# Routing ahead of an expert gather: eight choices taken early, sums of squares moved to VectorE, one head's weights moved behind

## The chip, the cores and the metric

The kernel runs on one core of a Trainium2 chip. Its engines are TensorE (matmuls; PE in the profile, its weight loads PEld), VectorE (DVE), ScalarE (ACT), GpSimd (POOL) and SyncE (SP). 16 DMA engines move data between HBM and SBUF; transfers are issued by SP, ACT and POOL. The metric is the device time of one execution in microseconds, lower is better; the kernel before has a median of 1541.05 us over three runs.

## The reference

One sequence of 256 tokens of width 1024 passes a first block (modulated norm, windowed attention beside a short convolution, then a PEER expert layer) and a second part with two attention layers and two gated feed-forward layers. All is float32. The change concerns the expert layer, `peer`, whose core is:

```python
qh = (t @ w_q).reshape(T, PEER_HEADS, 2, PEER_KEY_DIM // 2)
s = jnp.einsum('thpd,hpnd->thpn', qh, sub_keys)
s_top, i_top = lax.top_k(s, PEER_TOPK)
cand = s_top[:, :, 0, :, None] + s_top[:, :, 1, None, :]
best, pos = lax.top_k(cand.reshape(T, PEER_HEADS, 256), PEER_TOPK)
idx = take_along_axis(cand_idx, pos); g = softmax(best)
ue, ve = u_tab[idx], v_tab[idx]
act = gelu(einsum('thkd,td->thk', ue, t))
return einsum('thk,thkd->td', g * act, ve)
```

Here `t` is `h2 = rmsnorm(x, n2) * (1 + sc2) + sh2`, there are 8 heads, and each token picks 16 of 16384 experts for each head. Every pick needs a row of `u` and a row of `v`, 1024 floats each.

## The kernel before

The 256 tokens are two tiles of 128 (t = 0, 1). `phase_a` computes the first block up to the residual, `phase_b` the experts, `phase_c` the rest. A scheduler puts each engine's instructions in an order when the program is built; the order in the source is a priority, and `tc.issue_after(ins)` keeps what stands inside it behind `ins` on that engine's queue.

In `phase_b` a step `s` of 16 is one head for one token tile, and it has 16 choices `k`. So there are 256 choices, each one an indirect DMA issued by POOL (`fetch`, line 934): for each of 128 tokens it gathers one row of 8 KB, `u` and `v` side by side, into a place of a ring of `NR` = 13 places of 8 KB a partition (tag `uv`). `first` (line 939) takes the dot product of the `u` half with the tokens `ht` on VectorE and a GELU on ScalarE; `second` (line 948) scales an identity matrix by activation and softmax weight on VectorE (`dgw`) and adds the `v` half to four PSUM banks with eight products on TensorE. After `second` the place in the ring is free for the gather 13 choices on.

Before a step's choices stand, its indices are needed. `query(h)` projects the normed tokens `hf` with the head's weights `wq[h]` (`project`) and multiplies by the head's keys (`keys`). `routing(s)` then runs on VectorE in four steps: the best 16 of 128 scores for each half (`half`, with MAX8, FIND_INDEX8 and MATCH_REPLACE8, eight at a time), the best 16 of the 256 sums (`pairs`) and the decoding of their numbers into expert indices `IX[s]` (`decode`). In the loop of line 974 the steps of `routing(s + 2)` are dealt out at every fourth choice.

Head 0 goes a shorter way (`query_early`, line 848): its projection is made from `xg`, the tokens times the gain, before the norm is known; the scores are then scaled by the norm `rs` (its squares are summed in PSUM by 16 products with a column of ones in `square_sums`), and the shift's part, 16 products of the weights with the modulation column, then four with the keys, is added. `normed` builds `hf` with the norm spread over partitions (`spread`), `rows` transposes it into `ht`.

The weights of heads 0 to 3 are loaded into ring places ahead of any gather, those of heads 4 to 7 into stage buffers `raw`, `whi`, `wlo` (`qload`, line 773). All are issued on SP in turn. Queries 1 to 3 stand ahead of the loop, 4 to 7 at choices 8, 36, 68, 100; at choice 104 the prefetch of phase c's weights is allowed, at 120 `angles`, a small computation for phase c.

## Time and profile before

| | us |
|---|---|
| median of three runs | 1541.05 (1534.71 to 1544.97) |
| the profiled execution | 1528.92 |
| its span, first to last instruction | 1527.1 |
| TensorE busy / VectorE busy | 1384.6 / 1161.1 |
| ScalarE busy / POOL busy | 601.3 / 353.0 |
| mean granted clock of TensorE | 0.991 |

The busy share of an engine is taken over a program of stages with different limits, so it doesn't say what sets the time in a given stage. The page's row of DMA rates over 40 slices shows it better: slices 8 to 24 (some 270 to 920 us) move 376 to 427 GB/s, those of phase c mostly 100 to 200. The rows of a window are best read side by side: what each engine was busy, and what the DMA engines moved.

### The profile page before, as it was taken

The page shows a single profiled execution, that of the slowest core. Times are in us where ns is not written, and L with a number is a line of the kernel's source. Part 1 is how long each engine was busy: PE and PEld are TensorE (multiplying, and loading weights), DVE is VectorE, ACT ScalarE, POOL GpSimd, SP SyncE. Part 2 cuts the span into 40 slices and gives each one's busy share as a digit, 9 for nine tenths or more (in the row PEclk, how much of TensorE's full clock was granted, in tenths as well). Part 3 has the DMA queues.
Part 4 walks back from the last instruction along what each step waited for, and adds up shares of the span by engine and source line. Part 5 has one row for each costly group of instructions (what it writes and reads, how often), then busy time and mean ns, then how long its engine had stood idle before and what let it go on. Part 6 is the DMA issues. An engine that isn't in the chain of part 4 may idle for free.

```text
span 1527.1 us, 28521 instructions
## 1 busy us (share of the span) xinstructions
PE 1384.6 (91%) x10892; PEld 1294.2 (85%) x10892; DVE 1161.1 (76%) x2692; ACT 601.3 (39%) x1223; POOL 353.0 (23%) x316
## 2 busy tenths in 40 slices
PE   7999996999988887888688889999999999999998
PEld 7988896988987777777677779989999996899997
DVE  3887775996897779776565658876988888588885
ACT  1646633312111113111010005775655568555553
POOL 0000001343455455555455530000000000000000
PEclk9999998999999999999999999999999999999999
DMA  9677766999999999999999994434655543355550
GB/s 326 230 261 225 245 204 252 413 396 405 376 426 426 426 426 426 426 427 426 425 427 425 427 411 156 147 122 159 198 192 182 190 153 97 116 189 193 184 189 28
DMA packets 82839, 433.40 MB, mean 284 GB/s; under 512 B 9296, under 2 KB 10448, under 8 KB 49680
## 3 DMA queue, kind: packets, MB, share of 16 engines
q0 software_dynamic: 37120, 269.24, 42.4%
q1 hardware_dynamic: 43712, 159.67, 31.2%
q10 hardware_dynamic: 1872, 2.68, 0.5%
q8 instruction: 86, 1.41, 0.4%
q14 instruction: 49, 0.40, 0.1%
HBM read 430.51 MB, written 1.05 MB: 283 GB/s over the span
## 4 chain that ended last, share of the span: by engine, by line
PE 51%; DMA 31%; DVE 12%; issue 4%; ACT 1%; POOL 0%; SPq 0%; DVEq 0%; POOLq 0%; ACTq 0%
PE b L135 50%; DMA uv<-in_uv,IX 27%; DVE uv L944 2%; DMA rawx<-in_wmodT 1%; DVE wlo L212 1%; DVE dgw L953 1%; DMA rawx<-in_wmod 1%; DVE s L815 1%; DVE wlox L212 1%; DMA raw<-in_wmodT 1%; DMA raw<-in_wqkv 1%; DVE e L648 0%; DVE oh L916 0%; DVE rawx L477 0%; DVE SI L817 0%
## 5 line engine op out<-in xcount | busy, mean ns | idle before, releaser
L135 PE MATMUL b<-dgw,uv 128*128 128x128 f32 x4096 | 506.7, 279 | 98.9 <-DVE dgw L953 98.6
L135 PEld LDWEIGHTS b<-dgw,uv 128*128 128x128 f32 x4096 | 473.2, 192 | 133.7 <-DVE dgw L953 131.9
L944 DVE CUSTOM_DVE_ANT_0 uv<-uv,ht 128x1024 f32<-128x1024 f32 x256 | 312.7, 1221 | 142.1 <-DMA uv<-in_uv,IX 141.8
L936 POOL DMA_INDIRECT uv<-in_uv,IX x256 | 328.9, 1285 | 330.2 <-DMA uv<-in_uv,IX 141.6
L135 PE MATMUL b<-H,whi 128*128 128x256 f32 x1296 | 244.8, 287 | 2.7 <-DVE mx L1042 1.4
L945 ACT ACTIVATE act<-act 128x1 f32<-128x1 f32 x256 | 51.5, 202 | 496.7 <-DVE act L944 492.8
L135 PE MATMUL b<-H,wlox 128*128 128x256 f32 x824 | 231.9, 281 | 0.0
L135 PE MATMUL b<-H,whix 128*128 128x256 f32 x1216 | 222.9, 282 | 2.2 <-DVE H L535 1.1
L135 PEld LDWEIGHTS b<-H,whi 128*128 128x128 f32 x1296 | 201.6, 189 | 9.1 <-issue 5.0
L135 PEld LDWEIGHTS b<-H,whix 128*128 128x128 f32 x1216 | 187.8, 188 | 6.7 <-issue 3.2
L135 PEld LDWEIGHTS b<-H,wlox 128*128 128x128 f32 x824 | 155.6, 189 | 0.7 <-issue 0.3
L135 PE MATMUL b<-H,wlo 128*128 128x256 f32 x440 | 122.4, 288 | 0.0
L212 DVE TENSOR_TENSOR wlox<-rawx,whix 128x1024 fp32r<-128x1024 f32 x60 | 73.1, 1223 | 35.4 <-ACT whix L203 34.6
L953 DVE TENSOR_SCALAR dgw<-cn,act,we 128x128 f32<-128x128 f32 x256 | 88.0, 344 | 13.1 <-ACT act L945 13.1
L203 ACT ACTIVATE whix<-rawx 128x1024 fp32r<-128x1024 f32 x60 | 63.0, 1058 | 77.2 <-PE b L135 60.9
L203 ACT ACTIVATE whi<-rawx 128x1024 fp32r<-128x1024 f32 x59 | 62.3, 1059 | 66.2 <-PE b L135 61.3
L357 POOL TENSOR_TENSOR rs<-ms,nhalf 128x2 f32<-128x2 f32 x6 | 6.2, 1034 | 349.4 <-DVE ms L355 349.4
L212 DVE TENSOR_TENSOR wlox<-raw,whix 128x1024 fp32r<-128x1024 f32 x57 | 69.7, 1222 | 18.3 <-ACT whix L203 17.6
L135 PEld LDWEIGHTS b<-H,wlo 128*128 128x128 f32 x440 | 82.5, 189 | 1.2 <-issue 0.7
L203 ACT ACTIVATE whi<-raw 128x1024 fp32r<-128x1024 f32 x58 | 60.9, 1056 | 54.1 <-PE b L135 42.7
L203 ACT ACTIVATE whix<-raw 128x1024 fp32r<-128x1024 f32 x57 | 60.3, 1058 | 50.8 <-PE b L135 48.1
L1257 DVE SCALAR_TENSOR_TENSOR c<-u,cl,c 128x256 f32<-128x256 f32 x176 | 73.8, 479 | 0.8 <-ACT c L1254 0.7
(340 smaller groups left out, 2236.2 us busy)
## 6 DMA issues: line engine op xcount, KB each, us to landing
rawx<-in_wup SPq DMA_DIRECT2D x45, 512.0 KB, 3.5
raw<-in_wup SPq DMA_DIRECT2D x43, 512.0 KB, 3.5
raw<-in_wdn SPq DMA_DIRECT2D x23, 512.0 KB, 3.4
rawx<-in_win SPq DMA_DIRECT2D x21, 512.0 KB, 4.5
rawx<-in_wdn SPq DMA_DIRECT2D x21, 512.0 KB, 3.4
rawx<-in_wmodT SPq DMA_DIRECT2D x18, 512.0 KB, 4.5
raw<-in_wmodT SPq DMA_DIRECT2D x14, 512.0 KB, 4.4
raw<-in_win SPq DMA_DIRECT2D x13, 512.0 KB, 4.3
```

What stands on the lines that cost most here:

```text
L135: return self.nc.tensor.matmul(out, lhsT, rhs, start=start, stop=stop).ins
L203: nc.scalar.activation(hi[:], raw[:], AF.Copy)
L212: nc.vector.tensor_sub(u.lo[:], u.raw[:], u.hi[:].bitcast(F32))
L357: nc.gpsimd.tensor_tensor(rs[:], ms[:], self.nhalf[:, 0:2], OP.pow)
L815: nc.vector.match_replace(s2[:], v[:, 0:8], s, -3e38)
L936: nc.gpsimd.indirect_dma_start(out=g[:], out_offset=None, in_=A["uv"], in_offset=bass.IndirectOffsetOnAxis(ap=IX[s][:, k:k + 1], axis=0))
L944: dot = nc.vector.tensor_tensor_reduce(u, u, ht[:, t, :], 1.0, 0.0, OP.mult, OP.add, accum_out=a[:, 0:1]).ins
L945: nc.scalar.activation(a[:, 1:2], a[:, 0:1], AF.Gelu)
L953: done = nc.vector.tensor_scalar(dg[:], self.con("ident"), a[:, 1:2], e[:, k:k + 1], op0=OP.mult, op1=OP.mult).ins
L1257: nc.vector.scalar_tensor_tensor(c[:, a, :], u[:, a, j:j + 256], self.col("cw2", at + 44 * j), c[:, a, :], op0=OP.mult, op1=OP.add)
```

## The change

- `query_early` is put in another order: the shift's 16 products come first, and the projection is queued behind them. The squares are taken on ScalarE as before, but summed over four pairs of feature tiles by VectorE, so that 4 products with the column of ones remain of 16. Scaling by the norm and adding the shift are one VectorE instruction for each token tile, and the norm is spread here.
- `first8` (new) takes eight choices of step 0 from the best 8 of each half: 64 sums instead of 256. The first eight gathers use its indices, in the same order of choices. Then come `normed`, `rows`, and the rest of routing(0), which does not repeat the first MAX8 and FIND_INDEX8 of the halves; gathers 8 to 12 follow, then routing(1).
- `top8` and `parts` are split off `top16` and `decode`.
- Heads 0 to 2 have their weights in the ring, heads 3 to 6 in the stage buffers. Head 7 is loaded at choice 36, into the `raw` and `whi` that head 3 had. Queries 1 and 2 stand ahead of the loop, 3 to 7 at choices 8, 36, 68, 100, 132. The prefetch is allowed at 136 and `angles` at 144. The keys of head 1 are issued from ACT instead of POOL.
- A pad of 224 bytes stands in the pool below the ring. With the 32 bytes of the new tile `IX8` the ring's start moves by 256 bytes, from byte 111360 of a partition to 111616, which is a multiple of 512.

```diff
+            def qplace(h):
+                if h < 3:
                     g = rows_.tile([P, 2 * D], F32, name="wq", tag="uv", bufs=NR)
+                    wq[h] = [g[:, 0:D], g[:, D:2 * D]]
+                    return g
+                wq[h] = [self.slot("r", w, F32, "st") for w in
+                         ("wlo" if h == 6 else "raw", "wlo" if h == 6 else "whi")]
+            def qload(h, g=None):
+                if g is not None:
                     self.take(g[:].rearrange("p (u c) -> p u c", u=2), A["wpq"][2 * h:2 * h + 2].rearrange("u p c -> p u c"))
-                    wq[h] = [g[:, 0:D], g[:, D:2 * D]]
-                else:
-                    wq[h] = []
-                    for u in (2 * h, 2 * h + 1):
-                        g = self.slot("r", ["raw", "whi", "raw", "whi", "raw", "whi", "wlo", "wlo"][u - 8], F32, "st")
-                        self.take(g[:], A["wpq"][u])
-                        wq[h].append(g[:])
+                    return
+                for u in range(2):
+                    self.take(wq[h][u][:], A["wpq"][2 * h + u])
+            places = {h: qplace(h) for h in (0, 1, 2)}
             self.inturn = True
-            for h in range(8):
-                qload(h)
+            for h in range(7):
+                if h >= 3:
+                    qplace(h)
+                qload(h, places.get(h))
...
             def query_early():
-                ps = project(0, xg)
-                sums = self.square_sums(x)
-                rs = self.rms_col(sums)
-                sc, ks, end = keys(0, ps)
                 pc = self.rot("mm")
-                with self.tc.issue_after(end):
-                    for a in range(2):
-                        for k in range(KT):
-                            self.mm(pc[:, a * 128:a * 128 + 128], wq[0][a][:, k * 128:k * 128 + 128],
-                                    self.mod[:, 24 + k:25 + k].to_broadcast([P, 128]), k == 0 and a == 0, k == KT - 1 and a == 1)
+                for a in range(2):
+                    for k in range(KT):
+                        end = self.mm(pc[:, a * 128:a * 128 + 128], wq[0][a][:, k * 128:k * 128 + 128],
+                                      self.mod[:, 24 + k:25 + k].to_broadcast([P, 128]), k == 0 and a == 0, k == KT - 1 and a == 1)
                 cb = wk.tile([P, 256], F32, name="cb", tag="s2256", bufs=1)
                 nc.scalar.activation(cb[:], pc[:, 0:256], AF.Copy)
+                sq = [wk.tile([P, 512], F32, name="sq", tag=t, bufs=n) for t, n in [("oh", 1), ("qT", 2), ("qT", 2)]]
+                for b in range(4):
+                    q = sq[b] if b < 2 else sq[2]
+                    nc.scalar.activation(q[:], x[:, 2 * b:2 * b + 2, :].rearrange("p a t -> p (a t)"), AF.Square)
+                    if b:
+                        nc.vector.tensor_tensor(sq[0][:], sq[0][:], q[:], OP.add)
+                with self.tc.issue_after(end):
+                    ps = project(0, xg)
+                sums = self.rot("tr")
+                for h in range(2):
+                    for t in range(2):
+                        self.mm(sums[:, t:t + 1], sq[0][:, h * 256 + t * 128:h * 256 + t * 128 + 128], self.con("ones", 1),
+                                h == 0 and t == 0, h == 1 and t == 1)
+                rs = self.rms_col(sums)
+                ks = wk.tile([P, 256], F32, name="ks", tag="ks", bufs=2)
+                nc.gpsimd.dma_start(ks[:], A["keysT"][0])
                 pb = self.rot("mm")
                 for a in range(2):
                     self.mm(pb[:, a * 128:a * 128 + 128], cb[:, a * 128:a * 128 + 128], ks[:, a * 128:a * 128 + 128])
+                sc, _, _ = keys(0, ps, ks)
+                sb = wk.tile([P, 256], F32, name="sb", tag="cd", bufs=1)
+                nc.scalar.activation(sb[:], pb[:, 0:256], AF.Copy)
+                self.spread(rs, bc[:])
                 for t in range(2):
                     c = slice(t * 256, t * 256 + 256)
-                    nc.scalar.activation(scores[0][:, c], sc[:, c], AF.Copy, scale=rs[:, t:t + 1])
-                ss = scores[0][:].rearrange("p (t k) -> p t k", t=2)
-                nc.vector.tensor_tensor(ss, pb[:, 0:256].unsqueeze(1).to_broadcast([P, 2, 256]), ss, OP.add)
+                    nc.vector.scalar_tensor_tensor(scores[0][:, c], sc[:, c], rs[:, t:t + 1], sb[:], op0=OP.mult, op1=OP.add)
...
+            nc.vector.memset(wk.tile([P, 56], F32, name="pad")[:], 0.0)
...
+                def of(a):
+                    return scores[h][:, t * 256 + a * 128:t * 256 + a * 128 + 128]
                 def half(a):
+                    top16(SV[:, a, :], SI[:, a, :], of(a), 128, s == 0)
+                def parts(n, m, BI, bits, out):
+                    si = wk.tile([P, 2, m], F32, name="si", tag="si", bufs=1)
+                    nc.vector.tensor_scalar(si[:, 0, :], SI[:, 0, 0:m], 128.0, None, op0=OP.mult)
+                    nc.vector.tensor_copy(si[:, 1, :], SI[:, 1, 0:m])
+                    ab = wk.tile([P, 2, n], U32, name="ab", tag="ab", bufs=1)
+                    nc.vector.tensor_scalar(ab[:, 0, :], BI, bits, None, op0=OP.logical_shift_right)
+                    nc.vector.tensor_scalar(ab[:, 1, :], BI, m - 1, None, op0=OP.bitwise_and)
+                    af = wk.tile([P, 2, n], F32, name="af", tag="af", bufs=1)
+                    nc.vector.tensor_copy(af[:], ab[:])
+                    oh = wk.tile([P, 2, n, m], F32, name="oh", tag="oh", bufs=1)
+                    nc.vector.tensor_tensor(oh[:].rearrange("p a k c -> p (a k) c"),
+                                            self.con("iota", m).unsqueeze(1).to_broadcast([P, 2 * n, m]),
+                                            af[:].rearrange("p a k -> p (a k)").unsqueeze(2).to_broadcast([P, 2 * n, m]), OP.is_equal)
+                    nc.vector.tensor_tensor(oh[:], oh[:], si[:].unsqueeze(2).to_broadcast([P, 2, n, m]), OP.mult)
+                    ix = wk.tile([P, 2, n], F32, name="ixf", tag="ixf", bufs=1)
+                    nc.vector.tensor_reduce(ix[:], oh[:], mybir.AxisListType.X, OP.add)
+                    return nc.vector.tensor_tensor(out, ix[:, 0, :], ix[:, 1, :], OP.add).ins
+                def first8():
+                    for a in range(2):
+                        top8(SV[:, a, :], SI[:, a, :], of(a))
+                    cd = wk.tile([P, 64], F32, name="cd8", tag="s2128", bufs=1)
+                    nc.vector.tensor_tensor(cd[:].rearrange("p (a b) -> p a b", a=8),
+                                            SV[:, 0, 0:8].unsqueeze(2).to_broadcast([P, 8, 8]),
+                                            SV[:, 1, 0:8].unsqueeze(1).to_broadcast([P, 8, 8]), OP.add)
+                    top8(best, BI, cd[:])
+                    early.append(wk.tile([P, 8], U32, name="IX8"))
+                    return parts(8, 8, BI[:, 0:8], 3, early[0][:])
...
+            choices = [(s, k) for s in range(16) for k in range(16)]
+            query_early()
+            steps = routing(0)
+            last = steps.pop(0)()
+            for c in choices[0:8]:
+                fetch(*c)
             with self.tc.issue_after(last):
-                normed(rs)
+                normed()
                 rows()
+                for step in steps:
+                    last = step()
+            for c in choices[8:NR]:
+                fetch(*c)
+            with self.tc.issue_after(last):
                 for step in routing(1):
                     step()
-            choices = [(s, k) for s in range(16) for k in range(16)]
-            for c in choices[0:NR]:
-                fetch(*c)
-            for h in range(1, 4):
+            for h in range(1, 3):
...
-                if n in (8, 36, 68, 100):
-                    query(4 + n // 32)
-                if n == 104:
+                if n in (8, 36, 68, 100, 132):
+                    query(3 + n // 32)
+                if n == 36:
+                    qplace(7)
+                    qload(7)
+                if n == 136:
                     self.allowed = "ac"
                     self.fetch([])
-                if n == 120:
+                if n == 144:
```

## Rows read from the trace of the kernel before

**Rows 1.** The page's chain of work that ended last, shares of the span by line.

```profile
PE b L135 50%; DMA uv<-in_uv,IX 27%; DVE uv L944 2%; DMA rawx<-in_wmodT 1%; DVE wlo L212 1%; DVE dgw L953 1%; DMA rawx<-in_wmod 1%; DVE s L815 1%; DVE wlox L212 1%; DMA raw<-in_wmodT 1%; DMA raw<-in_wqkv 1%; DVE e L648 0%; DVE oh L916 0%; DVE rawx L477 0%; DVE SI L817 0%
```

**Rows 2.** Windows by stage: us, busy us per engine (instructions), granted clock, DMA share, GB/s.

```profile
218.00:233.00 15.00, 15.00 (x128) 15.00 (x128) 8.09 (x15) 5.79 (x10) 1.13 (x2) 1.00 0.08 30
...
233.00:252.00 19.00, 15.82 (x110) 14.61 (x108) 3.56 (x15) 4.49 (x10) 0.71 (x1) 1.00 1.00 392
252.00:260.00 8.00, 0.77 (x2) 0.50 (x2) 7.74 (x36) 0.40 (x2) 0.41 (x1) 0.56 0.01 5
...
270.00:290.00 20.00, 20.00 (x104) 17.48 (x102) 19.87 (x75) 8.12 (x18) 5.67 (x5) 1.00 1.02 425
290.00:330.00 40.00, 38.12 (x310) 36.98 (x309) 40.00 (x157) 11.42 (x25) 17.03 (x17) 1.00 0.98 386
...
370.00:410.00 40.00, 39.25 (x310) 37.93 (x309) 32.27 (x88) 9.22 (x25) 18.27 (x15) 1.00 0.97 360
410.00:910.00 500.00, 407.85 (x3267) 376.93 (x3265) 360.01 (x884) 76.50 (x248) 263.56 (x199) 1.00 1.01 426
910.00:925.00 15.00, 12.62 (x101) 11.58 (x101) 8.25 (x19) 1.22 (x6) 0.00 (x0) 1.00 0.40 169
```

**Rows 3.** The same view, two stretches of ten microseconds.

```profile
240.00:250.00 10.00, 8.82 (x73) 8.34 (x71) 0.76 (x2) 1.82 (x4) 0.71 (x1) 1.00 1.02 417
...
340.00:350.00 10.00, 9.73 (x67) 8.27 (x66) 9.83 (x37) 0.81 (x4) 4.79 (x3) 1.00 1.02 430
```

**Rows 4.** DMA view, 262 to 925 us: totals; issues with KB, us to landing.

```profile
DMA packets 38777, 273.93 MB, mean 413 GB/s; under 512 B 4304, under 2 KB 4944, under 8 KB 5968
...
uv<-in_uv,IX POOLq DMA_INDIRECT x254, 18.8
raw<-in_wqkv SPq DMA_DIRECT2D x5, 512.0 KB, 9.0
rawx<-in_wqkv SPq DMA_DIRECT2D x3, 512.0 KB, 12.3
```

**Rows 5.** Timeline of TensorE: start us, us, instruction, count, idle time before it.

```profile
233.81 7.15 PE L135 MATMUL b<-H,wq 128*128 128x256 f32 x32
240.80 2.73 PE L135 MATMUL b<-cn,sq 128*128 128x1 f32 x24
243.40 1.14 PE L135 MATMUL b<-ks,qT 128*128 128x128 f32 x8
244.37 3.74 PE L135 MATMUL b<-mod,wq 128*128 128x128 f32 x32
248.58 0.71 PE L135 MATMUL b<-ks,cb 128*128 128x128 f32 x4 [0.47 <-ACT cb L862]
```

**Rows 6.** Timeline of VectorE, the first routing.

```profile
250.13 0.49 DVE L813 MAX8 SV<-ss 128x8 f32<-128x128 f32 x2
...
251.32 0.28 DVE L816 MAX8 SV<-s 128x8 f32<-128x128 f32 x1
251.70 0.28 DVE L817 FIND_INDEX8 SI<-SV,s 128x8 uint32<-128x128 f32 x1
...
253.02 0.41 DVE L896 TENSOR_TENSOR cd<-SV 128x256 f32<-128x256 f32 x1
...
256.34 0.69 DVE L916 TENSOR_TENSOR oh<-cn,af 128x512 f32<-128x512 f32 x1
...
258.52 0.18 DVE L923 TENSOR_TENSOR IX<-ixf 128x16 uint32<-128x16 f32 x1
```

**Rows 7.** Timeline of POOL: two gathers.

```profile
259.59 1.06 POOL L936 DMA_INDIRECT uv<-in_uv,IX  x1 [15.05 <-DVE SV L813]
...
316.69 1.05 POOL L936 DMA_INDIRECT uv<-in_uv,IX  x1 [9.21 <-PE b L135]
```

**Rows 8.** Waits of POOL, 262 to 925 us: in total, times, longest.

```profile
POOL uv L936 <- PE b L135: 86.9, 47, 9.2
```

**Rows 9.** Waits of ScalarE, 340 to 400 us: in total, times, longest.

```profile
ACT whi L203 <- DMA raw<-in_wqkv: 8.3, 2, 6.1
```

More of the change, by code (lines that the diff above doesn't have):

```diff
@@ L799, in phase_b @@
             self.resid(x, self.big, g1, gained, sums=None)
-            ht = rows_.tile([P, 2, D], F32, name="ht")
+            ht = []
             def rows():
+                ht.append(rows_.tile([P, 2, D], F32, name="ht", tag="ht", bufs=1))
                 for t in range(2):
@@ L808, in rows, with top8, top16 @@
                             nc.tensor.transpose(ps[:, k * 128:k * 128 + 128], hf[:, 4 * h + k, t * 128:t * 128 + 128], self.con("ident"))
-                        nc.scalar.activation(ht[:, t, h * 512:h * 512 + 512], ps[:], AF.Copy)
-            def top16(v, idx, s, n):
-                s2 = wk.tile([P, n], F32, name="s2", tag=f"s2{n}", bufs=1)
+                        nc.scalar.activation(ht[0][:, t, h * 512:h * 512 + 512], ps[:], AF.Copy)
+            def top8(v, idx, s):
                 nc.vector.max(v[:, 0:8], s)
                 nc.vector.max_index(idx[:, 0:8], v[:, 0:8], s)
+            def top16(v, idx, s, n, begun=False):
+                s2 = wk.tile([P, n], F32, name="s2", tag=f"s2{n}", bufs=1)
+                if not begun:
+                    top8(v, idx, s)
                 nc.vector.match_replace(s2[:], v[:, 0:8], s, -3e38)
@@ L827, in project, with keys @@
                 return ps
-            def keys(h, ps):
-                ks = wk.tile([P, 256], F32, name="ks", tag="ks", bufs=2)
-                nc.gpsimd.dma_start(ks[:], A["keysT"][h]) if h < 2 else nc.scalar.dma_start(ks[:], A["keysT"][h])
+            def keys(h, ps, ks=None):
+                if ks is None:
+                    ks = wk.tile([P, 256], F32, name="ks", tag="ks", bufs=2)
+                    nc.scalar.dma_start(ks[:], A["keysT"][h])
                 qt = wk.tile([P, 2, T], F32, name="qT", tag="qT", bufs=2)
@@ L878, in normed @@
                     nc.scalar.activation(hf[:, k, :], t2[:], AF.Identity, bias=self.mod[:, 24 + k:25 + k])
-            IX, WT = {}, {}
+            nc.vector.memset(wk.tile([P, 56], F32, name="pad")[:], 0.0)
+            IX, WT, early = {}, {}, []
             def routing(s):
@@ L906, in decode @@
                 def decode():
[L907 to L921 removed]
                     IX[s] = wk.tile([P, 16], U32, name="IX", tag="IX", bufs=4)
[L923 removed]
+                    last = parts(16, 16, BI[:], 4, IX[s][:])
                     e = WT[s]
@@ L927, in decode @@
                     return last
-                return [lambda: half(0), lambda: half(1), pairs, decode]
+                return [first8] * (s == 0) + [lambda: half(0), lambda: half(1), pairs, decode]
             big = self.bigs()
@@ L936, in fetch @@
                 nc.gpsimd.indirect_dma_start(out=g[:], out_offset=None, in_=A["uv"],
-                                             in_offset=bass.IndirectOffsetOnAxis(ap=IX[s][:, k:k + 1], axis=0))
+                                             in_offset=bass.IndirectOffsetOnAxis(
+                                                 ap=early[0][:, k:k + 1] if s == 0 and k < 8 else IX[s][:, k:k + 1], axis=0))
             def first(s, k):
@@ L943, in first @@
                 u = ring[s, k][:, 0:D]
-                dot = nc.vector.tensor_tensor_reduce(u, u, ht[:, t, :], 1.0, 0.0, OP.mult, OP.add, accum_out=a[:, 0:1]).ins
+                dot = nc.vector.tensor_tensor_reduce(u, u, ht[0][:, t, :], 1.0, 0.0, OP.mult, OP.add, accum_out=a[:, 0:1]).ins
                 nc.scalar.activation(a[:, 1:2], a[:, 0:1], AF.Gelu)
@@ L959, in second @@
                 return done
-            rs = query_early()
-            for step in routing(0):
-                last = step()
+            choices = [(s, k) for s in range(16) for k in range(16)]
[4 more added lines that the diff above has]
+                fetch(*c)
             with self.tc.issue_after(last):
-                normed(rs)
+                normed()
                 rows()
+                for step in steps:
[3 more added lines that the diff above has]
+            with self.tc.issue_after(last):
                 for step in routing(1):
                     step()
-            choices = [(s, k) for s in range(16) for k in range(16)]
-            for c in choices[0:NR]:
-                fetch(*c)
-            for h in range(1, 4):
+            for h in range(1, 3):
                 query(h)
```

24 lines of the change are left out of this document (2 added, 22 removed).

## The prediction

> **What bounds the kernel now.** I read the page's chain of work first. Two names carry it: TensorE's matmuls of line 135 with half of the span, and the gathers of expert rows, `uv<-in_uv,IX`, with 27% [rows 1]. Everything in the diff lies in phase b, the expert phase, or just ahead of it, so I cut that part into stages with the windows view [rows 2]. The reader is to see four things there. From 218 to 233 us the DMA engines are almost idle while TensorE finishes phase a. From 233 to 252 they load the query weights. From 252 to 260 they stand still again: 0.01 busy, while VectorE works 7.74 of 8 us on the first routing. From 270 they are full, and in the 500 us from 410 to 910 they move 426 GB/s at a share of 1.01 while TensorE and VectorE have room. So the end of phase b is set by the bytes of the gathers, by when they start, and by the bytes that fail to move in between.
>
> The DMA view of 262 to 925 us gives the bytes: 273.93 MB [rows 4]. At 426 GB/s that is 643.0 us. From 262 to the last transfer (910 plus 0.40 x 15 us of share, so about 916) [rows 2] is 654 us. So some 11 us are lost inside the stretch. The windows say where: 290 to 330 at 386 GB/s loses 3.8 us, 370 to 410 at 360 GB/s loses 6.2 us. The waits of POOL say why: POOL, which issues the gathers, waited 86.9 us for TensorE, that is for a free place in the ring of 13 [rows 8]. One gather, for example, went out at 316.69 after 9.21 us of such a wait [rows 7]. All those losses are paid before 410; after that only bytes count.
>
> One gather is 1.049 MB, so 2.46 us at 426 GB/s.
>
> **The change part by part, on the path to the first gather.** Before, VectorE starts its first MAX8 at 250.13 and ends the indices IX at 258.70, and POOL issues the first gather at 259.59 [rows 6, 7].
>
> *Scores.* TensorE's order before is: project from 233.81 for 7.15 us, 24 small products of the squares for 2.73 us, keys 1.14 us, shift products 3.74 us, a copy on ScalarE, then 0.71 us for the last four [rows 5]. After, the shift products come first, at the end of phase a's matmuls (about 233.0), since TensorE has no gap before it [rows 2, 5]. So they delay the projection: 233.0 + 3.74 + 7.15 = 243.9. Of the 32 products of squares 8 are left, at 2.73/24 us each 0.9 us, and the 0.71 us of the shift follow them, so TensorE is busy while ScalarE copies the projection (a copy of half that size cost TensorE 0.47 us of idle time in front of the last row of [rows 5]; I estimate 0.8 us). Keys then run from about 245.5 to 246.7, the two VectorE instructions that scale and add take about 1 us (two halves of the 0.69 us instruction that they replace, plus a fixed part), and MAX8 starts at about 247.8: **2.3 us earlier**. The sums of squares on VectorE (three additions, 0.69 us each by the 512-element rows [rows 6]) fall where VectorE is idle, 3.56 of 19 us busy [rows 2], so I cost them at nothing; without that cover they would cost 2.1 us. The spread of the norm moves ahead too and hides behind the keys.
>
> *Eight choices first.* The full first routing takes 258.70 - 250.13 = 8.57 us. The new `first8` needs two MAX8 and two FIND_INDEX8 over 128 elements (0.28 us each; with their value loads about 1.3 us), a sum over 64 pairs, a MAX8 and a FIND_INDEX8 over 64 (about 0.85 us), two shifts and a cast (0.5 us), three passes over 128 elements where the row has 512 (0.69 us; by 0.41 us for 256 an element costs 1.1 ns, so 384 fewer leave 0.27 us, 0.9 us for three with their hand-overs) and the last addition 0.18 us [rows 6]. That is 3.8 us, so **4.7 us earlier**. Together the first gather is issued at about 252.6, **7.0 us earlier**, and seven heads' weights instead of eight are off the DMA engines by about 249.5, so nothing is in its way.
>
> *The rest of the first tile.* Choices 8 and on need the full routing: eight products for the normed rows (about 3 us) and the remaining 7.3 us of routing, so IX at about 262. The eight gathers keep the DMA engines busy until 254.3 + 8 x 2.46 = 274. No gap. VectorE does about 2.6 us more than before (the pairs, the search and the decoding of eight). It is busy without a break from 270 to 330 [rows 2], so this work is not free there; what it costs in the ring is the first rival.
>
> *The weights of the last head.* They were loaded ahead of the gathers, when the DMA engines were free; now, at choice 36, 1.049 MB join a full stretch. In that stretch the DMA engines have a share of 1.01 [rows 2], and loads of half the size took 9.0 and 12.3 us to land [rows 4]. I cost the move at its bytes, **2.46 us later**; its lower bound is 0, if it falls in one of the 11 us of gaps. The Trainium skill (DMA: Bandwidth & Descriptors, section "Issuing engines are not separate DMA queues") says that DMAs issued from different engines end up on the same 16 DMA engines and interleave. By that rule the full 2.46 us are due and the sum is -4.5; if the load had room of its own the sum would be -7.0. The trace agrees with the rule.
>
> *The ring's place.* A pad of 224 bytes and the new 32-byte tile move the ring by 256 bytes, from an odd multiple of 256 to a multiple of 512. No row shows a gather at another place, so I bound it by saturated stretches whose transfers go elsewhere: 417 GB/s from 240 to 250 (weights into three other buffers) and 430 from 340 to 350 [rows 3]. Over the gathers' 630 us these would make +13.6 and -5.9 us. I take nothing: both rows also hold other traffic, and 500 us of gathers at 426 lie between them.
>
> *Queries.* Two heads instead of three are projected ahead of the loop, so TensorE can start on the first choice about 8 us sooner (7.15 + 1.14). But little was lost there: 425 GB/s from 270 to 290 [rows 2]. The same number of queries, seven, still has to pass through TensorE early. I cost this at nothing.
>
> **Sum.** -2.3 - 4.7 + 2.46 = **-4.5 us**, the 11 us of gaps unchanged. Against the profiled execution (1528.92 us, span 1527.1) that is 1524.4 us. The runs shown have their median at 1541.05, 12 us above the profiled one, and I put the difference on the median: **1536.5 us**.
>
> **The rivals.**
>
> *The ring swallows the start.* A gather needs a place that an earlier choice has left, and between 262 and 410 the places come from work that is itself full: VectorE 40.00 of 40 us from 290 to 330, TensorE 38.12 there and 39.25 from 370 to 410 [rows 2]. VectorE starts 2.3 us earlier but has 2.6 us more to do. If the place of gather 50 is left when it was before, the 7 us only fill the ring sooner, and the DMA engines wait 7 us more. Since 2.46 us of load then fall in the gaps, the time is that of before: 1541, from 1539 to 1543. For it: the 86.9 us of waits [rows 8]. Against it: VectorE from 290 on also did routing well ahead of need (nearly all 40 us busy against 360 of 500 later), so it has work that can give way.
>
> *The gaps close too.* The first choice starts sooner on TensorE, the queries are spread over 132 choices instead of 100, and the prefetch of phase c moves later. If this removes half to all of the 11 us, it is -10 to -15.5: 1525.5 to 1531. Against it: the prefetch and the queries run when their buffers come free, not when their line is reached: ScalarE waited for `raw<-in_wqkv` between 340 and 400 [rows 9], long before choice 104.
>
> *Slower: a late load in front of TensorE.* The last head's weights can only be loaded when head 3's place is free, and take 9.0 to 12.3 us to land in a full stretch [rows 4]. If TensorE's queue has the last query within some 10 us behind that, everything behind it waits: the matmuls of the choices, then the ring, then the gathers. TensorE has no slack before 410. Price 9 to 12.3 us, less 4.5: +4.5 to +8, so 1545.5 to 1549. The like of it is in the trace: ScalarE's waits for `raw<-in_wqkv` came to 8.3 us, the longest 6.1 [rows 9]. It decides only if the query stands that close behind its load; the diff puts a hundred choices between them.
>
> *The place in memory matters.* By the bounds above, 1531 to 1550. For it speaks no row but those two.
>
> **How the numbers follow.** The forecast, -2 to -7 us, has 45 in 100; the swallowed start 22; the closed gaps 15; the late load 13; the place 5. The time is the forecast's, 1536.5. Medians of three moved within 10 us here, so 8 in 10 needs some 4 us beyond the cases: from 1525 to 1549, which leaves out part of the closed gaps, the worse half of the place in memory and the top of the late load. The forecast's own range is 1532 to 1541. Faster by over 1% (below 1525.6, about what a measurement can tell) takes nearly all gaps closed: 0.10. Slower by over 1% (above 1556.5) takes a late load and a swallowed start together: 0.07. Within 1%: 0.83.
>
> **What would show it.** Right: first MAX8 near 248, first gather issued near 252.6, 426 GB/s from 410 on, and the last dot product near 916.5 instead of 921. Wrong: POOL's waits for TensorE grow by about the 7 us gained (first rival); the windows from 290 to 410 near 426 GB/s (second); TensorE idle for a load of the last head (third); another rate than 426 in the long stretch (fourth). The sum fails at its root if the shift products do not start right behind phase a's matmuls.

## The result and the profile after

The changed kernel takes 1521.37 us (median of 4, 1520.72 to 1522.44), the kernel before took 1543.01 beside it (1534.71 to 1545.38): a ratio of 0.9878 with a 95% interval of 0.9851 to 0.9905 (the two medians by themselves give 0.9860). The forecast was 1536.5, from 1525 to 1549: faster than forecast, and below the range. In two later series of runs, beside the kernel before, the ratio was 0.9921 (0.9897 to 0.9944) and 0.9909 (0.9891 to 0.9926). The profiled executions differ by less: 1521.2 against 1528.92 us, spans 1519.1 and 1527.1.

The start of the expert phase after the change: TensorE, VectorE and POOL in the timeline view (start us, us, instruction, count, idle time before it). The first row is the last product of phase a.

```profile
233.82 0.28 PE L135 MATMUL b<-mh,wlox 128*128 128x256 f32 x1
233.94 3.74 PE L135 MATMUL b<-mod,wq 128*128 128x128 f32 x32
237.52 7.07 PE L135 MATMUL b<-H,wq 128*128 128x256 f32 x32
244.43 0.95 PE L135 MATMUL b<-cn,sq 128*128 128x1 f32 x8
...
247.72 0.48 DVE L820 MAX8 SV<-ss 128x8 f32<-128x128 f32 x2
...
252.07 1.07 POOL L982 DMA_INDIRECT uv<-in_uv,IX  x1 [5.69 <-DVE s L827]
...
264.54 0.94 POOL L982 DMA_INDIRECT uv<-in_uv,IX  x1 [1.14 <-DVE SV L820]
...
912.97 1.23 DVE L991 CUSTOM_DVE_ANT_0 uv<-uv,ht 128x1024 f32<-128x1024 f32 x1 [0.94 <-DMA uv<-in_uv,IX]
```

The shift products start right behind phase a, the first MAX8 stands at 247.72 instead of 250.13 [rows 6], the first gather at 252.07 instead of 259.59 [rows 7]. Gather 8, the first that needs the full routing, goes out at 264.54 after an idle time of 1.14 us. The last dot product starts at 912.97; 916.5 was forecast.

The same stages in the windows view of the changed kernel (columns as in [rows 2]):

```profile
252.00:260.00 8.00, 7.95 (x30) 6.13 (x31) 7.15 (x30) 5.79 (x13) 6.41 (x6) 0.61 0.73 258
...
290.00:330.00 40.00, 37.74 (x269) 34.28 (x268) 39.98 (x154) 9.62 (x22) 16.02 (x13) 1.00 1.01 424
330.00:370.00 40.00, 37.79 (x266) 34.09 (x265) 31.10 (x104) 7.83 (x21) 15.72 (x12) 1.00 1.01 411
370.00:410.00 40.00, 40.00 (x334) 39.20 (x333) 38.58 (x118) 10.39 (x28) 20.74 (x18) 1.00 0.97 370
410.00:890.00 480.00, 391.82 (x3106) 362.40 (x3104) 341.76 (x835) 71.93 (x236) 252.87 (x192) 0.99 1.01 426
```

From 252 to 260 the DMA engines now move 258 GB/s where they stood still. Of the two stalls of [rows 2] the one in 290 to 330 is gone (424 instead of 386 GB/s); the other is there (411 and 370). Against 426 GB/s the three windows lose 0.2 + 1.4 + 5.3 = 6.9 us; before, 290 to 330 and 370 to 410 lost 10.0. In the long stretch the rate is 426 as before. POOL's waits for TensorE from 262 to 925 us came to 83.7 us, against 86.9 [rows 8].

### The profile page after: what moved, and what is told of

Read it like the earlier page. It is cut to its first block, busy times and chain, and to the rows that moved or that the text cites. A ratio compares the mean times of both kernels' runs of the same rounds, so it can differ in the third digit from the quotient of the medians.

```text
span 1519.1 us, 28502 instructions
## 1 busy us (share of the span) xinstructions
PE 1384.9 (91%) x10868; PEld 1293.2 (85%) x10868; DVE 1163.0 (77%) x2710; ACT 603.1 (40%) x1224; POOL 354.7 (23%) x315
## 4 chain that ended last, share of the span: by engine, by line
PE 48%; DMA 32%; DVE 13%; issue 5%; ACT 1%; POOL 0%; SPq 0%; DVEq 0%; POOLq 0%; ACTq 0%
PE b L135 47%; DMA uv<-in_uv,IX 28%; DVE uv L991 2%; DMA rawx<-in_wmodT 2%; DMA rawx<-in_wmod 1%; DMA raw<-in_wmodT 1%; DVE dgw L1000 1%; DVE wlox L212 1%; DVE wlo L212 1%; DVE s L827 1%; DMA raw<-in_wqkv 0%; DVE raw L477 0%; DVE oh L938 0%; DVE e L648 0%; ACT whi L203 0%
## 5 line engine op out<-in xcount | busy, mean ns | idle before, releaser
L135 PE MATMUL b<-H,whi 128*128 128x256 f32 x1312 | 248.9, 288 | 2.7 <-DVE mx L1097 1.4
```

The costliest lines, as they stand in the source:

```text
L135: return self.nc.tensor.matmul(out, lhsT, rhs, start=start, stop=stop).ins
```

## The experiments

Each run is read by three stretches, from the timeline views: from the start of phase a's last product to the issue of the first gather; from there to the last dot product (the row behind it that stores its sum, 922.33 before and 914.12 after); from there to the end of the span. In us:

| kernel | phase a's last product | to first gather | gathers | after last dot | median of its runs |
|---|---|---|---|---|---|
| before | 232.88 | 26.71 | 662.7 | 604.8 | 1541.05 |
| before_again | 233.47 | 28.33 | 662.9 | 604.6 | 1531.13, one run |
| before_ring512 | 233.80 | 28.33 | 662.7 | 603.1 | 1532.95 |
| before_moved512 | 232.63 | 26.70 | 663.8 | 609.1 | 1533.54 |
| b_warm | 233.04 | 26.70 | 667.7 | 607.8 | 1540.23 |
| b_held | 232.05 | 28.33 | 655.2 | 604.5 | 1524.35 |
| after | 233.82 | 18.25 | 662.0 | 605.0 | 1521.37 |
| after_again | 232.00 | 18.24 | 661.8 | 609.8 | 1521.91 |
| after_beside | 233.81 | 18.25 | 661.9 | 603.2 | 1523.32 |
| after_ring256 | 232.70 | 18.24 | 662.7 | 607.7 | 1523.23 |
| after_nopad | 233.43 | 18.24 | 671.6 | 609.4 | 1534.98 |
| a_full_first | 235.44 | 23.39 | 662.2 | 606.8 | 1529.1 |
| a_old_scores | 234.84 | 23.23 | 660.8 | 605.2 | 1526.71 |
| a_old_weights | 236.64 | 18.19 | 664.2 | 607.6 | 1523.42 |
| old_w_q4_held | 236.27 | 18.19 | 665.6 | 607.6 | 1530.1 |
| a_late_queries | 233.28 | 18.24 | 662.2 | 608.0 | 1524.87 |
| a_q3_first | 235.91 | 18.24 | 662.0 | 603.2 | 1524.28 |
| a_held | 233.13 | 18.25 | 657.7 | 609.3 | 1519.85 |
| a_held_old_w | 234.87 | 18.19 | 656.0 | 603.0 | 1514.0 |
| held_old_w_beside | 234.48 | 18.20 | 656.5 | 609.4 | 1517.56 |

The first column and the last stretch belong to code that no edit touches, and still vary by 4.6 and 6.8 us; in the three profiles of the changed kernel alone by 1.8 and 6.5. So single times scatter by some 10 us. Of one kernel the two middle stretches repeat within about a microsecond, but for the two values of the old start, of which more below. What makes the last stretch vary can be read from the traces. Two profiles of the changed kernel, after_again and after_beside, over the same 160 us of work, from 290 us behind the last dot product:

```profile
1202.00:1362.00 160.00, 156.33 (x1183) 140.58 (x1182) 121.89 (x293) 101.38 (x221) 5.46 (x12) 0.96 0.40 138
```

```profile
1204.00:1364.00 160.00, 156.33 (x1231) 142.54 (x1230) 127.86 (x306) 105.70 (x227) 5.38 (x12) 1.00 0.42 143
```

The granted clock of TensorE (1.00 is full speed) was 0.96 in the first, whose last stretch took 609.8 us, and 1.00 in the second, with 603.2. All twenty profiles follow it: the clock missing there, 1 less the granted clock, times 160 us, is 0 in the four of 603.0 to 603.2, 1.6 us in the five of 604.5 to 605.2, 3.2 in the one of 606.8, 4.8 in the five of 607.6 to 608.0 and 6.4 in the five of 609.1 to 609.8. Medians are only compared within a series, run on one chip; the kernel before had a median of 1535.38 beside the four ring kernels, 1536.66 beside the three kernels with one part undone and b_warm, 1533.2 beside after_again, a_late_queries and a_q3_first, 1533.77 beside the three held kernels, 1538.59 beside after_beside and held_old_w_beside, 1537.39 beside old_w_q4_held.

**The ring's place.** A line `nc.vector.memset(wk.tile([P, n], F32, name="pad")[:], 0.0)` ahead of the ring moves it: n = 64 or 128 in the kernel before, n = 120 or none in the changed one (56).

> The kernel before with a pad of 256 bytes below the ring and nothing else, so that the ring starts at a multiple of 512 bytes as in the changed kernel. Theory A (the place of the ring costs time in the runs that are timed without a profile): the runs close up near the profiled time of before, 1528 to 1531 us, 10 to 15 us under its median of 1543. Theory B (the change's gain lies in the order of work, and the spread of the runs of before has another cause): within 2 us of the median of before, with the same spread of some 10 us.

> The kernel before with a pad of 512 bytes: the ring moves as a pad moves it, but stays at an odd multiple of 256. Theory A: as before, about 1541, with its spread. Theory B: as before too. If moving the ring at all is what helps: 1528 to 1531.

> The changed kernel with a pad of 480 instead of 224 bytes, so that the ring starts at an odd multiple of 256. Theory A: 10 to 15 us slower than the changed kernel, 1531 to 1536, with a spread of some 10 us between runs. Theory B: 1521, as the changed kernel.

> The changed kernel without the pad: the ring starts at byte 111392, which is 288 bytes over a multiple of 512 and 32 over a multiple of 256. Theory A: slower than the changed kernel by as much as at an odd multiple of 256 or more, 1531 to 1545. Theory B: 1521.

Ratios to the kernel before: 0.9982 (0.997 to 0.9993), 0.9984 (0.9966 to 1.0002), 0.9914 (0.9898 to 0.993), 0.9993 (0.998 to 1.0007). Theory A falls: the kernel before gained the same 0.2% from either pad, and the changed kernel lost none of its gain at an odd multiple of 256. Only after_nopad lies where A put it, and its ring starts at no multiple of 256. The gathers' long stretch in the windows view, first after_ring256, then after_nopad:

```profile
410.00:890.00 480.00, 391.83 (x3103) 362.14 (x3103) 340.96 (x830) 71.93 (x236) 251.22 (x192) 0.99 1.01 426
```

```profile
410.00:890.00 480.00, 381.95 (x3049) 352.06 (x3048) 335.56 (x821) 71.11 (x232) 247.19 (x188) 1.00 1.01 419
```

An odd or even multiple of 256 bytes makes no difference (426 GB/s in all). 32 bytes beyond a multiple, where the tile IX8 alone would put the ring, makes it 419, and 662.7 become 671.6 us. So the pad wins nothing over the kernel before, whose ring lay at a multiple of 256 already; it keeps about 9 us from being lost. The Trainium skill (DMA: Bandwidth & Descriptors, section "How a descriptor splits into AXI transactions") says that a transaction must begin at a 256-byte boundary, so that a descriptor beginning elsewhere needs an extra, partly unused one. The lower rate has the direction of that rule; but the page speaks of bytes that are fetched, while here the place written to moved, so that no run here shows this to be the cause.

**One part undone.** first8 left out (whole routing, then all gathers); the old order of the first scores; the old places, order and loads of the weights.

> The changed kernel without first8: the whole routing of the first tile runs before the first gather, as in the kernel before; the early shift products, the squares on VectorE, the placing of the weights and the ring at a multiple of 512 bytes stay. Theory START (all of the gain is that the gathers start earlier, about 4.7 us of it by first8): first gather near 257, last dot near 917.5 to 918, 1525.5 to 1528. Theory CLOCK (TensorE's long idle stretch in the first routing lets its clock fall, and what that costs differs between executions; it is what makes the kernel before spread from 1527 to 1540): the idle stretch is back to some 9 us, so the spread is back as well, with times from 1524 to 1537 and a median of 1530 or more. Theory PLACES (the gain beyond the start is that three, not four, of the 13 ring places hold weights at first): 1525 to 1528 with the narrow spread of the changed kernel.

> The changed kernel with the first scores as the kernel before makes them: projection first, squares summed in PSUM, the shift products last, the scaling on ScalarE and one sum on VectorE, the spread of the norm after the routing. first8, the weights and the ring's place stay. Theory START: first MAX8 near 250.1, first gather near 254.5, 1523.5 to 1526 (2.3 us over the changed kernel). Theory CLOCK: TensorE then idles from 249.3 to the spread of the norm, some 5 us as in the changed kernel, so the narrow spread stays, 1523.5 to 1526. Theory PLACES: the same. If the scores are hidden by something else, 1521 to 1523.

> The changed kernel with the weights of the queries as in the kernel before: eight heads loaded ahead of the gathers, four of them in ring places, queries 1 to 3 ahead of the loop, the later ones after choices 8, 36, 68 and 100, the first units of the last stage after 104. Early scores, first8 and the ring at a multiple of 512 bytes stay. Theory PLACES: gathers 10 to 13 wait for the queries again, 290 to 330 falls from 424 towards 386 GB/s, the time is 1526 to 1532 and the spread of the kernel before comes back. Theory START: the 2.46 us of head 7's weights leave the full stretch and go to the time before the gathers, where the DMA is idle anyway: 1519 to 1521.5. Theory CLOCK: as the changed kernel, 1519 to 1524, narrow.

Without first8 the first gather stands 23.39 us behind phase a instead of 18.24 (+5.15), with the old scores 23.23 (+5.0); the gathers' stretch stays within 1.2 us. The old weights don't touch the start but lengthen the gathers by 2.2 us, though they take head 7's loads out of them; the three windows from 290 to 410:

```profile
290.00:330.00 40.00, 36.01 (x289) 34.61 (x287) 40.00 (x151) 11.17 (x25) 20.11 (x17) 1.00 1.01 423
330.00:370.00 40.00, 39.07 (x273) 35.29 (x274) 32.23 (x117) 5.26 (x17) 17.73 (x13) 1.00 1.00 400
370.00:410.00 40.00, 36.51 (x295) 34.62 (x294) 33.51 (x93) 11.00 (x28) 19.24 (x15) 1.00 0.88 335
```

The last two lose 10.9 us (2.4 + 8.5), against 6.7 in the changed kernel; from 290 to 330 nothing is lost, so PLACES has fallen for that window: with the early start the stall of the kernel before stays away there with four ring places too. START holds for the first two by their stretches, and the sum, 10.15, is what lies between 18.24 and the 28.33 of three of the six profiles with the old start. The other three have 26.7. The difference, 1.6 us (in a_old_scores too), is TensorE's clock. before_ring512's timeline:

```profile
244.32 1.14 PE L135 MATMUL b<-ks,qT 128*128 128x128 f32 x8
245.29 5.37 PE L135 MATMUL b<-mod,wq 128*128 128x128 f32 x32
```

Its windows view, the first 4 us of these:

```profile
244.00:248.00 4.00, 4.00 (x27) 4.00 (x27) 0.16 (x1) 0.84 (x2) 0.71 (x1) 0.69 1.03 423
```

Behind the 24 one-column products of the squares [rows 5] the granted clock was 0.69 here, and the shift products took 5.37 us; at 1.00 they took 3.74. In all twelve profiles with the new order and first8 the first gather stood at 18.2. The medians of the three kernels are less clean: all three lie above START's ranges, by 0.7 to 1.9 us, and a_full_first spread by 10.8 us, as CLOCK had it; the changed kernel itself later spread by 8.5.

**TensorE's clock in the idle stretch.** Eleven products whose result nothing reads, behind the first scores of the kernel before:

```diff
+def warm():
+    ps = self.rot("mm")
+    for _ in range(11):
+        self.mm(ps[:], self.con("ident"), x[:, 0:2, :].rearrange("p a t -> p (a t)"))
...
 rs = query_early()
+warm()
```

> The kernel before with 11 products of 128 by 512 on TensorE, whose result nothing reads, behind the first scores (249.3 to about 258.7), where it idles for 9.94 us; nothing else is changed. Theory CLOCK: the granted clock stays near 1.00 from 249 to 270 (0.50 to 0.68 from 252 to 268 without it), the spread of 1527 to 1540 shrinks to some 3 us and the median falls by 5 to 10 us, to 1525 to 1530. Theories START and PLACES: TensorE gains up to 4 us of its work near 260, but the gathers start no earlier; median 1532 to 1536 with the spread as it was.

The clock was higher (1.00 from 252 to 260, 0.83 from there to 270; 0.56 and 0.67 before) and the kernel was slower, 1.0031 (1.0015 to 1.0046), with the gathers 5 us longer. CLOCK falls: the low clock in that gap is not what costs the kernel before its time. Of the 5 us, 3.6 are more of the stalls from 290 to 410 (13.6 us lost there, 10.0 before); why these products lengthen them wasn't settled.

**What stalls the gathers from 290 to 410.** First the queries' places in the source:

```diff
-if n in (8, 36, 68, 100, 132):
-    query(3 + n // 32)
-if n == 36:
+if n in (40, 64, 88, 112, 132):
+    query((40, 64, 88, 112, 132).index(n) + 3)
+if n == 44:
     qplace(7)
     qload(7)
```

a_q3_first puts query 3 ahead of the loop, with queries 1 and 2.

> The changed kernel with queries 3 to 7 after choices 40, 64, 88, 112 and 132 (instead of 8, 36, 68, 100, 132) and head 7's loads after 44; nothing else. Theory BACKLOG (the gathers stall between 290 and 410 because TensorE has queries as well as choices to do, 7 us of products for each query, so that ring places come free late; the three heads in the ring and query 3 behind choice 8 already closed a part of it): the gaps of the changed kernel between 330 and 410, 1.4 + 5.2 us, shrink to 2 at most, the last dot moves from 913.3 to 908 to 909.5, 1515 to 1518.5 us. Theory START (the gain is that the gathers start earlier, and nothing else): the gaps only move, to where the queries now are, 1520 to 1524.

> The changed kernel with query 3 ahead of the choices (queries 1 to 3, as in the kernel before) instead of after choice 8; its weights stay out of the ring, three heads stay in ring places, head 7's loads stay after choice 36. Theory BACKLOG: TensorE begins the choices 7 to 8 us later, the stall moves into 290 to 330 (below 400 GB/s), about as much of it in all or up to 3 us more: 1521 to 1526. Theory PLACES (it is the fourth ring place that head 3 held which stalled the kernel before in 290 to 330): 290 to 330 stays at 420 GB/s or more, 1520 to 1523.

Both came out like the changed kernel (662.2 and 662.0), the first because its edit hardly reached the chip: a place in the source is only a priority. TensorE's last query ended at 386.9 us there and at 387.0 in the changed kernel, by the timelines. The second did move query 3 ahead, and that made no difference: one query more or less ahead of the choices isn't it. Then the queries were tied to TensorE's own queue:

```diff
-self.mm(big[b][:, ...
+self.behind = self.mm(big[b][:, ...
...
-if n in (8, 36, 68, 100, 132):
-    query(3 + n // 32)
-if n == 36:
+if n in (40, 64, 88, 112, 132):
+    with self.tc.issue_after(self.behind):
+        query((40, 64, 88, 112, 132).index(n) + 3)
+if n == 44:
     qplace(7)
     qload(7)
```

This is a_held. b_held does it in the kernel before, and a_held_old_w in the changed kernel with the old weights, both with queries 4 to 7 at choices 40, 64, 84 and 100.

> The changed kernel with queries 3 to 7 really held: their products stand behind the products of choices 39, 63, 87, 111 and 131 in TensorE's queue (in a_late_queries the builder had moved queries 4 to 7 ahead again, so that they ran where they run in the changed kernel, one or two pairs of products behind each choice up to 386 us); head 7's loads after choice 44. Theory BACKLOG (the gathers stall between 290 and 410 because TensorE has the queries to do besides the choices, 3.1 instead of 2.0 us for each choice): the stall of 6.6 us in 330 to 410 shrinks to 2 at most, both stretches are at 420 GB/s or more, the stretch from the end of the stage before the scores to the last dot falls from 680.4 to 675 to 677, 1516 to 1519 us where the changed kernel takes 1522. Theory START (only the start of the gathers counts, the stall is set by something else): 680 to 681, the changed kernel's time.

> The kernel before with queries 4 to 7 held in the same way, behind choices 39, 63, 83 and 99; nothing else. Theory BACKLOG: of its stalls, 4 us in 290 to 330 and 6 to 7 in 370 to 410, the second closes and the first stays (queries 1 to 3 and the fourth ring place are as they were): 684 to 686 from the end of the stage before to the last dot instead of 689.5 to 691.2, and 4 to 6 us off the time of the kernel before. Theory START: no change.

> The changed kernel with the weights as in the kernel before (eight heads loaded ahead, four of them in ring places, queries 1 to 3 ahead of the choices) and queries 4 to 7 held behind choices 39, 63, 83 and 99. Theory BACKLOG: the 2.46 us of head 7's loads leave the full stretch, as the prediction priced them, and the stall that ate them in a_old_weights (335 GB/s in 370 to 410) is gone: 673 to 676 us from the end of the stage before to the last dot, 2 us less than a_held unless query 3 and the fourth ring place stall the gathers in 290 to 330. Theory PLACES (the fourth ring place stalls them): 677 to 680, 290 to 330 below 410 GB/s. Theory START: 682, as a_old_weights.

Ratios to the kernel before: 0.9899 (0.9872 to 0.9926), 0.9937 (0.9913 to 0.996), 0.9878 (0.9852 to 0.9904). b_held's windows:

```profile
290.00:330.00 40.00, 34.21 (x293) 32.94 (x292) 40.00 (x159) 9.45 (x22) 22.65 (x19) 1.00 1.01 425
330.00:370.00 40.00, 35.79 (x311) 35.03 (x312) 39.57 (x106) 7.23 (x25) 25.55 (x19) 1.00 1.01 425
370.00:410.00 40.00, 33.60 (x259) 31.63 (x258) 29.29 (x96) 7.52 (x20) 18.19 (x14) 1.00 1.01 425
```

Both stalls of the kernel before are gone, against 386 and 360 GB/s in [rows 2], with ring places and query loads untouched; TensorE is 33.60 instead of 39.25 us busy in the last window. POOL's waits for TensorE from 290 to 410 us (in total, times, longest), first the kernel before, then b_held:

```profile
POOL uv L936 <- PE b L135: 54.5, 25, 9.2
```

```profile
POOL uv L936 <- PE b L135: 25.8, 20, 7.0
```

And TensorE's timeline of the kernel before shows how the queries delay the choices:

```profile
389.54 1.46 PE L135 MATMUL b<-H,wlo 128*128 128x256 f32 x6
390.84 1.95 PE L135 MATMUL b<-dgw,uv 128*128 128x128 f32 x16
```

A piece of a query stands between the products of one choice (`dgw,uv`) and the next, so that a choice comes every 3.09 us, while a gather moves in 2.46. BACKLOG stands: TensorE, with queries and choices at once, gave the ring's places back too late. Busy alone is no sign of it: a_held's TensorE was busy 40.00 of 40 us from 330 to 370 at 426 GB/s. Holding the queries also moved the first steps of phase c, which use the queries' buffers: before, three loads of its weights were issued from 311.74 on, in b_held one by 420, at 381.35, and with them went 2.36 us of VectorE between 370 and 410. What that adds wasn't tried alone. b_held closed more than expected: 7.5 us (662.7 to 655.2) instead of 4 to 6, the stall in 290 to 330 too.

The two stall-free kernels also give the price of head 7's loads by itself: 657.7 (a_held, inside the stretch) less 655.2 (b_held, ahead of it) is 2.5 us. a_held_old_w has them ahead as well, and one stall of 2.3 us left, from 330 to 370 (402 GB/s). PLACES has fallen there too: 426 GB/s from 290 to 330.

Last, why moving the weights made the stalls smaller although it moved no query later:

> The kernel of a_old_weights (the changed kernel with the weights as in the kernel before) with query 4 alone held behind choice 19, where the changed kernel has it; there it ran behind choice 8. The fourth ring place stays with head 3. If it is the one query more among the first choices that makes the larger stall of a_old_weights (400 and 335 GB/s in 330 to 370 and 370 to 410): 330 to 410 as in the changed kernel, 405 and 370 or more, and 659 to 661.5 us from the first gather to the last dot instead of 664.2. If it is the fourth ring place: 663.5 to 665, as in a_old_weights.

665.6, with 384 and 339 GB/s in the two windows: not query 4. The number is near the 663.5 to 665 of the fourth ring place, but that place alone stalled nothing in 290 to 330 in a_held_old_w (426 GB/s). Also different is when phase c's weights are loaded (from 304 us on in a_old_weights, from 326 in the changed kernel). Against this cause speaks old_w_q4_held itself: it loaded them from 329 us on and stalled more. What it is stays open.

**The gain, and the best version.**

> The changed kernel itself, beside the others on this chip. If its executions are as close together on every chip as on the first two (1520.7 to 1522.4 and, with the ring at an odd multiple of 256, 1522.7 to 1524.1): 1520 to 1524 and 12 to 15 us below the kernel before. If its gain is the sum of what the single parts cost when they were undone (5.0 + 3.5 + 1.8 us from the end of the stage before the scores to the last dot): 9 to 12 us below the kernel before, with a spread of some 6 us.

> The kernel before itself, for one more profile of it: the end of the stage before the scores (232.6 to 233.8 us in three profiles of its like, 232.6 to 236.6 in all), the stretch from there to the last dot (689.5 to 691.0) and the stretch after the last dot (603.1 to 609.2). If the spread of its times lies ahead of the scores and after the last dot, where nothing was changed, the middle stretch is 689 to 692 us here too, whatever the time is; if it lies in the middle stretch (TensorE's clock in the idle stretch), that is 689 to 698.

> The changed kernel itself on one more chip, beside a_held_old_w's kernel and the kernel before. From the profiles so far the stretch from the end of the stage before the scores to the last dot is 680.0 to 680.9 us here and 689.5 to 691.2 in the kernel before: 9 to 12 us below it. If the 21.6 us of the first comparison belong to the change and not to the draws there: 18 us or more below it.

> The kernel of a_held_old_w again, beside the changed kernel on the same chip: 6 to 7 us below the changed kernel (674 against 680.4 us from the end of the stage before the scores to the last dot), 16 to 20 us below the kernel before.

The changed kernel was 11.3 us below the kernel before in the one and 15.3 us in the other, with spreads of 8.5 and 8.6 us (1516.53 to 1525.03; 1519.31 to 1527.88): its narrow spread at first was chance. Of the second comparison 9 to 12 us were expected if the stretches tell all, 18 or more if the first result does; it came out between. The two middle stretches of the changed kernel sum to 680.1 to 680.3 us, those of before and before_again to 689.5 and 691.2. The kernel of a_held_old_w was 5.8 us below the changed kernel on one chip, 1517.56 against 1523.32, and 0.9858 (0.9839 to 0.9878) of the kernel before, 21.0 us below it: it beats both. Both differences lie a little beside what was expected (6 to 7 and 16 to 20 us).

## Why the prediction was wrong

*Scores and first8: right in mechanism, small in size.* From phase a's last product, MAX8 came 17.25 us later before and 13.90 after: 3.35 us, not 2.3. The working took phase a to end at 233.0 in both; it ended 0.94 us later in the profile after, so the absolute 247.72 met the forecast 247.8 by that shift, which was luck. The working added TensorE's rows whole, but each starts some 0.15 us before the one ahead of it ends (237.52 against 233.94 + 3.74, for one), 0.6 us over the four steps up to the keys. first8 gave 5.1 us instead of 4.7. Together 8.5 instead of 7.0, and 10.1 where the old order meets a low clock, which the one profile of before didn't show.

*The first gains reach the end.* They do: undoing either leaves the gathers' stretch within 1.2 us of itself. The rival that the ring swallows the start has fallen, and its sign, 7 us more of POOL's waits for TensorE, did not come (83.7 against 86.9). Only beside the old weights is a part swallowed: a_old_weights took 664.2 us where the kernel before took 662.7, 1.5 us of the start.

*The last head's weights.* 2.46 us was forecast and 2.5 measured (a_held against b_held). The rule of the Trainium skill that speaks for the full price (DMA: Bandwidth & Descriptors, "Issuing engines are not separate DMA queues") agrees. The rival of a late load in front of TensorE has fallen: head 7's loads were issued at 294.99 and 295.76 us, the last query ended at 387.0, and TensorE's waits from 290 to 410 name no load.

*"The 11 us of gaps unchanged": the step that failed.* The windows lost 10.0 us before and 6.9 after, 3.1 us less, which paid for head 7's loads: the gathers' stretch came out 0.7 us shorter (662.7 to 662.0) instead of 2.46 longer. By the single parts: 1.5 us lost by the early start beside the old weights, 2.2 won by the new weights, places and queries. What sets the gaps is where the queries stand in TensorE's queue, with what moves along with them: b_held, which changes nothing else, closed them wholly. The second rival had the mechanism (the gaps close too), though it priced 5.5 to 11 us, and the prediction gave it 15 in 100. Its objection, that queries run when their buffers come free and not when their line is reached, was right, as a_late_queries shows; it did not follow that the stalls stay.

*The ring's place: nothing, rightly.* 426 GB/s. The bounds of +13.6 and -5.9 us, from stretches with other traffic, were wide of this move, but not of a move by 32 bytes.

*"I put the difference on the median".* Sum by the measured terms: -8.5 - 0.7 = -9.2 us between the two profiles' stretches, 4.7 more than forecast. The forecast missed by 15.1 us. The other 10.4 us are outside these stretches, and the base is the second step that failed: 1541.05 was the median of three runs, and in the later series the same kernel had medians of 1533.2 to 1538.59, 2.5 to 7.9 us lower; the rest is not explained. Either error alone would have left the time inside the range: 1531.8 with the measured sum, 1526.1 with a base 10.4 us lower. Against the profile the working was nearer: 1524.4 us forecast, 1521.2 measured. The scatter goes with TensorE's clock. Over the 100 executions of the kernel before in the later series the mean granted clock lies between 0.985 and 0.992, and the time follows it: 1541.4 us in the mean of the four at 0.985, 1531.3 of the fifteen at 0.991, which was the clock of the profile in the prediction. So that profile was a fast draw, and a median of 1541 is what executions at the low end take; the clocks of those three runs are not on record. Why the clock differs between executions, and why the later medians differ by 11 to 15 us where the stretches differ by 9 to 11, stays open, since those runs have no stages.

## What to carry to other kernels

Before a stall in a stretch bound by transfers is called unchanged, ask which engine gives the buffers back and what else stands in its queue: work with a later due time (here queries) belongs behind a named instruction of that engine's own queue, since a place in the source is only a priority. Price a change by the stretches between fixed events, which repeat within a microsecond here, and forecast a median from the spread of many runs, not from three, with their granted clocks beside the times. A small tile added below a ring of gather buffers can cost bandwidth, as the 32 bytes here did: look at where the ring then starts.

## What was unexpected of the hardware

A start 32 bytes beyond a multiple of 256 took gathers of 8 KB rows from 426 to 419 GB/s; 256 against 512 bytes did nothing. The clock of TensorE fell behind a run of one-column products in some executions of the same program and not in others (shift products 3.74 or 5.37 us). In phase c, too, the granted clock differed between executions of one program: 0.96 in after_again, 1.00 in after_beside over the same 160 us of work (the rows stand under the table), 6.4 us of missing clock against the 6.5 us between their last stretches, 609.8 and 603.2.
